# Two layers of a hybrid trunk: the step-size chain's products issued with the z products

## The chip, the cores and the metric

The kernel runs on one core of a Trainium2 chip. The metric is the device time of one execution in microseconds, over several runs. Four compute engines matter here: TensorE (PE) multiplies matrices, VectorE (DVE) and ScalarE (ACT) do the elementwise work, and SyncE (SP) starts the DMAs that bring the weights from HBM. GpSimd (POOL) has almost nothing to do.

## The reference

Each of two layers is a half-step SwiGLU feed-forward block, a mixer and a second feed-forward block, on 256 tokens of width 1024 in float32. The mixer has one input projection, whose columns are z, xBC, dt, q, k and v. Of its two halves the first is a Mamba-2 scan in chunks of 128 tokens, and the step sizes, with which this change deals, belong to it (cut to what matters):

```python
xbc = jax.nn.silu(causal_depthwise_conv(xbc, conv_w[i], conv_b[i]))
dt = jax.nn.softplus(dt_raw + dt_bias)            # 16 heads, 256 tokens
a = -jnp.exp(a_log)
adt = dt * a
a_cum = jnp.cumsum(adt, axis=-1)                  # within a chunk
lmat = jnp.exp(segment differences of a_cum, causal)
y_diag = cb * lmat * X                            # X = x * dt
decay_states = jnp.exp(a_cum[..., -1:] - a_cum)   # the kernel's dec, first chunk
states = Bc, decay_states, X
y_off = Cc, previous state, exp(a_cum)            # the kernel's dec, second chunk
```

The other half is attention: q and k are normalised per head with an RMS norm, scores are masked in three dilated windows, and their softmax weighs v. Both halves side by side go through the output projection.

## The kernel before, in words

Every big product is made three times, from a high and a low part of the weights and of the activations (L250 to L252, or the same sum in another order). The weights come in halves of 128x1024. For each half ScalarE casts the high part (L166, `wh`) and VectorE subtracts it from the weights to get the low part (L168, `wl`). The mixer's halves go through a ring of five slots, r0 to r4. In the stage of q, k and v a half serves 12 products of 512 columns, four halves serve a block of 512 output columns, and a slot is written again five halves later, so the cast of a half waits for the last product that reads the slot's old content.

The order of the mixer's products is: z with dt (the z stage), xBC with the convolutions, then first halves of q, k and v, second halves of q, k and v, and the output projection. Each block of q, k or v goes into a pair of PSUM tiles (`mm_pair`), one tile for each half of the tokens. Work that depends on finished blocks runs in generators ("threads"): `spawn` puts one on a list, `tick` (once for a step of the products) lets each go on to its next `yield`, and `after(events)` yields until the named events have been added. The SSD work (`group_in`, `decay_mask`, `group_out`), the normalising of q and k (`qk_norm_T`) and the attention (`head_pair`) are such threads. The order of the source is a priority only: a scheduler then places each instruction in its engine's queue by its own estimate of when its operands are there, so that an instruction can stand ahead of one that the source gives earlier.

The step-size chain (`step_sizes`, L521) computes dt as a softplus by an exponential and a series on VectorE (L525 to L541), adt and its high and low parts (L543 to L546), two small products that sum adt along the tokens (`pd`, L550 and L551), the exponential of the sums (`dec`, L552), and the first chunk's product of dec and dt (`dtd`, L553). The event "dt" lets `group_in` go on to `xe` (L619), and `decay_mask` begin. In `qk_norm_T`, L736 and L737 make the sums of squares, `rsqrt` (L223 to L236) their reciprocal roots, L742 the normalised q or k, and L749 transposes these on TensorE.

```python
def after(*evs):
    while not all(e in events for e in evs):
        yield 1
```

Of the kernel before, what the change touches and what calls it, by code (L numbers as in the profile page):

```python
# [18 lines left out]
AF = mybir.ActivationFunctionType  # L19
# [33 lines left out]
def tile_hybrid_trunk(ctx: ExitStack, tc: tile.TileContext, x, w_ffn_in, w_ffn_down, w_z, w_dtz,  # L53
                      w_xbc, w_qkv, w_out, norms, conv_wb, head_par, qk_norm, consts, out):
    nc = tc.nc
    vec, act, pool, pe = nc.vector, nc.scalar, nc.gpsimd, nc.tensor
# [151 lines left out]
# [3 lines that stand above are left out]
# [290 lines left out]
    def mixer(layer, xT, xn, norm, tail):  # L501
# [15 lines left out]
        dec = sm.tile(sh, F32, tag="dec", name="dec")  # L517
# [2 lines left out]

        def step_sizes():  # L521

            yield from after(*[f"xbc{j}" for j in range(8)])
            e = sm.tile(sh, F32, tag="sp_e", name="sp_e")
            vec.scalar_tensor_tensor(e, u, -1.0, u, op0=OP.mult, op1=OP.min)  # L525
            first = act.activation(e, e, AF.Exp)
            with tc.issue_after(first.ins):
                act.activation(ea, hpar[:, layer, 1, :], AF.Exp)
            yield 1
            s = sm.tile(sh, F32, tag="sp_s", name="sp_s")  # L530
            vec.tensor_scalar(s, e, 2.0, None, op0=OP.add)
            vec.reciprocal(s, s)
            vec.tensor_tensor(s, s, e, op=OP.mult)
            s2 = sm.tile(sh, F32, tag="sp_s2", name="sp_s2")
            vec.tensor_tensor(s2, s, s, op=OP.mult)
            a = sm.tile(sh, F32, tag="sp_a", name="sp_a")
            vec.tensor_scalar(a, s2, 1.0 / 15, None, op0=OP.mult)
            for n in (13, 11, 9, 7, 5, 3):
                vec.scalar_tensor_tensor(a, a, 1.0 / n, s2, op0=OP.add, op1=OP.mult)
            vec.scalar_tensor_tensor(a, a, 1.0, s, op0=OP.add, op1=OP.mult)  # L540
            vec.tensor_scalar(dt, u, 0.0, None, op0=OP.max)  # L541
            vec.scalar_tensor_tensor(dt, a, 2.0, dt, op0=OP.mult, op1=OP.add)
            vec.scalar_tensor_tensor(adt, dt, -1.0, ea[:, None, :].to_broadcast(sh),  # L543
                                     op0=OP.mult, op1=OP.mult)
            vec.tensor_copy(adh, adt)
            vec.tensor_tensor(adl, adt, adh.bitcast(F32), op=OP.subtract)  # L546
            yield 1

            pd = pt.tile(sh, F32, tag="s", name="pd")
            pe.matmul(pd[:, 0, :], low, adt[:, 0, :], start=True, stop=True)  # L550
            pe.matmul(pd[:, 1, :], tri, adt[:, 1, :], start=True, stop=True)  # L551
            act.activation(dec, pd, AF.Exp)  # L552
            vec.tensor_tensor(dtd, dec[:, 0, :], dt[:, 0, :], op=OP.mult)  # L553
            events.add("dt")

        a2, z1 = [st.take(), st.take()], [st.take(), st.take()]
        for t in range(2):
# [6 lines left out]
            unit_first(256, xT, t, z1, p1[:, :256])  # L564
            act.activation(zs[t][:, 512:768], p1[:, :256], AF.Silu)
        spawn(step_sizes())
        pz = mm_pair("pz", 512)
        unit_tok(512, 2, xT, pz)
# [385 lines left out]
```

## Time and profile before

| | |
|---|---|
| median of 3 runs | 1228.69 us (1228.65 to 1229.54) |
| profiled execution | 1229.02 us |
| its span on the core | 1227.2 us |
| TensorE busy | 1219.2 us |
| VectorE busy | 780.7 us |
| ScalarE busy | 686.2 us |
| mean granted clock of TensorE | 0.999 |

The profiled execution is one run; its span is the time between the first and the last instruction in the trace. A busy share is a mean over stages. Layer 1's z stage lies from about 197 to 221.5 us of the span, its convolutions to 269, its stage of q, k and v to 376.5, and the output projection to 428; layer 2's stage of q, k and v lies from 876 to 983. Times below are us from the span's start.

### The profile page before, as it was taken

The numbers are of one execution on the slowest core, as the hardware profiler recorded it, in microseconds if no ns is written. First come the engines' busy times: TensorE is split into PE (matmuls) and PEld (weight loads), VectorE is DVE, ScalarE is ACT, GpSimd is POOL, SyncE is SP. The second block draws the span as 40 slices with busy tenths as digits, with TensorE's granted clock in tenths as the row PEclk, the third lists the DMA queues.
The fourth block names the chain that finished last, engine by engine and source line by source line (L and its number), as shares of the span: only waits on it lengthen the run. The fifth ranks groups of instructions, "written<-read, shape, count | busy, mean of one in ns | idle before, by whom it ended". The sixth has DMA issues, their size and how long they took to land.

```text
span 1227.2 us, 16729 instructions
## 1 busy us (share of the span) xinstructions
PE 1219.2 (99%) x6191; PEld 1018.2 (83%) x6191; DVE 780.7 (64%) x1389; ACT 686.2 (56%) x1118; POOL 7.3 (1%) x14
## 2 busy tenths in 40 slices
PE   9999999999999999999999999999999999999998
PEld 6888888998877888888888888889988778888887
DVE  6755546788796586554385554478887875755541
ACT  6654435677866465544364543366769674644440
POOL 0000000000000000000000000000000000000000
PEclk9999999999999999999999999999999999999999
DMA  8855553654334466555456554645533344755550
GB/s 297 265 181 187 185 192 105 205 178 136 111 126 135 156 222 206 188 185 181 150 202 211 189 184 142 208 143 190 183 120 104 120 130 144 268 185 184 188 171 35
DMA packets 58833, 211.48 MB, mean 172 GB/s; under 512 B 6784, under 2 KB 7040, under 8 KB 58752
## 3 DMA queue, kind: packets, MB, share of 16 engines
q1 hardware_dynamic: 58032, 208.24, 50.2%
q0 software_dynamic: 576, 2.10, 0.5%
q8 instruction: 49, 0.80, 0.3%
q14 instruction: 32, 0.26, 0.1%
q10 hardware_dynamic: 144, 0.08, 0.0%
HBM read 209.34 MB, written 1.05 MB: 171 GB/s over the span
## 4 chain that ended last, share of the span: by engine, by line
PE 97%; DVE 1%; ACT 1%; DMA 1%; issue 0%; SPq 0%
PE pgu L250 13%; PE pgu L252 13%; PE pgu L251 13%; PE acc L250 9%; PE acc L251 9%; PE acc L252 9%; PE pq L252 3%; PE pq L250 3%; PE pq L251 3%; PE pc L252 3%; PE pc L250 3%; PE pc L251 3%; PE tr L467 2%; PE pz L250 1%; PE pz L251 1%; PE psc L783 1%
## 5 line engine op out<-in xcount | busy, mean ns | idle before, releaser
L168 DVE TENSOR_TENSOR wl<-w,wh 128x1024 fp32r<-128x1024 f32 x268 | 327.4, 1224 | 190.7 <-ACT wh L166 188.1
L166 ACT CAST wh<-w 128x1024 fp32r<-128x1024 f32 x268 | 280.6, 1052 | 225.1 <-PE pgu L252 71.8
L168 DVE TENSOR_TENSOR we<-w,we 128x1024 fp32r<-128x1024 f32 x124 | 151.2, 1225 | 126.1 <-ACT we L166 124.7
L166 ACT CAST we<-w 128x1024 fp32r<-128x1024 f32 x124 | 130.1, 1054 | 131.5 <-PE pgu L252 62.6
L250 PE MATMUL pgu<-wh,xTh 128*128 128x512 f32 x384 | 151.9, 396 | 0.1
L251 PE MATMUL pgu<-wl,xTh 128*128 128x512 f32 x384 | 149.6, 390 | 0.0
L252 PE MATMUL pgu<-wh,xTl 128*128 128x512 f32 x384 | 149.3, 390 | 0.0
L250 PE MATMUL pgu<-we,xTh 128*128 128x512 f32 x312 | 123.3, 395 | 0.0
L251 PE MATMUL pgu<-we,xTh 128*128 128x512 f32 x312 | 121.5, 390 | 0.0
L252 PE MATMUL pgu<-we,xTl 128*128 128x512 f32 x312 | 121.4, 390 | 0.0
L252 PEld LDWEIGHTS pgu<-wh,xTl 128*128 128x128 f32 x384 | 72.1, 188 | 15.3
L250 PEld LDWEIGHTS pgu<-wh,xTh 128*128 128x128 f32 x384 | 72.1, 188 | 15.0 <-ACT xTh L286 0.8
L251 PEld LDWEIGHTS pgu<-wl,xTh 128*128 128x128 f32 x384 | 72.2, 188 | 14.3
L250 PE MATMUL pq<-wh,xTh 128*128 128x512 f32 x192 | 78.8, 410 | 0.0
L252 PE MATMUL pq<-wh,xTl 128*128 128x512 f32 x192 | 78.2, 407 | 0.0
L251 PE MATMUL pq<-wl,xTh 128*128 128x512 f32 x192 | 78.2, 407 | 0.0
L250 PE MATMUL pc<-xTh,wh 128*128 128x256 f32 x256 | 72.9, 285 | 0.0
L252 PE MATMUL pc<-xTh,wl 128*128 128x256 f32 x256 | 72.4, 283 | 0.0
L251 PE MATMUL pc<-xTl,wh 128*128 128x256 f32 x256 | 72.4, 283 | 0.0
L252 PEld LDWEIGHTS pgu<-we,xTl 128*128 128x128 f32 x312 | 58.6, 188 | 12.5
L250 PEld LDWEIGHTS pgu<-we,xTh 128*128 128x128 f32 x312 | 58.6, 188 | 11.9 <-ACT xTh L286 0.3
L251 PEld LDWEIGHTS pgu<-we,xTh 128*128 128x128 f32 x312 | 58.6, 188 | 11.7
(209 smaller groups left out, 2259.7 us busy)
## 6 DMA issues: line engine op xcount, KB each, us to landing
w<-in_w_ffn_in_dram SPq DMA_DIRECT2D x176, 512.0 KB, 4.6
w<-in_w_ffn_down_dram SPq DMA_DIRECT2D x88, 512.0 KB, 3.7
w<-in_w_qkv_dram SPq DMA_DIRECT2D x48, 512.0 KB, 3.6
w<-in_w_xbc_dram SPq DMA_DIRECT2D x32, 512.0 KB, 4.3
w<-in_w_out_dram SPq DMA_DIRECT2D x32, 512.0 KB, 3.7
w<-in_w_z_dram SPq DMA_DIRECT2D x12, 512.0 KB, 4.9
w<-in_w_dtz_dram SPq DMA_DIRECT2D x4, 544.0 KB, 5.1
nw<-in_norms_dram POOLq DMA_DIRECT2D x4, 512.0 KB, 4.6
```

What stands on the lines that cost most here:

```text
L166: self.high = act.copy(h, src)
L168: self.low = vec.tensor_tensor(l, src, h.bitcast(F32), op=OP.subtract)
L250: pe.matmul(o, ah, bh, start=first, stop=False)
L251: pe.matmul(o, ah, bl, start=False, stop=False)
L252: guard["pe"] = pe.matmul(o, al, bh, start=False, stop=last)
L467: pe.transpose(p[:, i, tok(t)], h[:, t, i * 128:(i + 1) * 128], ident)
L783: pe.matmul(p[:, 0:256], qT[:, pr, 128:256], kz[:, pr % 4, i, :], start=True, stop=True)
```

## The change

The wait for the convolutions' events no longer stands at the head of the chain but between the pd products and the exponential of dec. The sums are copied out of PSUM by VectorE, and the exponential works in place on the copy.

```diff
@@ -520,7 +520,6 @@
 
         def step_sizes():
 
-            yield from after(*[f"xbc{j}" for j in range(8)])
             e = sm.tile(sh, F32, tag="sp_e", name="sp_e")
             vec.scalar_tensor_tensor(e, u, -1.0, u, op0=OP.mult, op1=OP.min)
             first = act.activation(e, e, AF.Exp)
@@ -549,7 +548,9 @@
             pd = pt.tile(sh, F32, tag="s", name="pd")
             pe.matmul(pd[:, 0, :], low, adt[:, 0, :], start=True, stop=True)
             pe.matmul(pd[:, 1, :], tri, adt[:, 1, :], start=True, stop=True)
-            act.activation(dec, pd, AF.Exp)
+            vec.tensor_copy(dec, pd)
+            yield from after(*[f"xbc{j}" for j in range(8)])
+            act.activation(dec, dec, AF.Exp)
             vec.tensor_tensor(dtd, dec[:, 0, :], dt[:, 0, :], op=OP.mult)
             events.add("dt")
 
```

Lines from L524 to L550 of the new file are the old L525 to L551; the copy is L551, the exponential L553, dtd L554, and later lines are the old number plus 1.

What this makes of the queues differs in three places. ScalarE's queue in the z stage of layer 1, before the change (`ea` is the exponential of a_log, `zv` the activation of z, ACT_TABLE_LOAD the loading of a function's table):

```order
L565 ACT_TABLE_LOAD
L565 ACTIVATE zv<-pz_1705 128x256
L166 CAST wh<-w 128x1024
L528 ACT_TABLE_LOAD
L528 ACTIVATE ea<-hpar 128x16
L166 CAST wh<-w 128x1024 x2
L570 ACT_TABLE_LOAD
L570 ACTIVATE zv<-pz_1781 128x512
L166 CAST wh<-w 128x1024
```

And after it:

```order
L566 ACT_TABLE_LOAD
L566 ACTIVATE zv<-pz_1705 128x256
L527 ACT_TABLE_LOAD
L527 ACTIVATE ea<-hpar 128x16
L166 CAST wh<-w 128x1024 x2
L553 ACTIVATE dec<-dec 128x32
L166 CAST wh<-w 128x1024
L571 ACT_TABLE_LOAD
L571 ACTIVATE zv<-pz_1781 128x512
```

The exponential of dec now stands in the z stage, behind that of ea and with no load of its own, and ea with its load stands one cast earlier.

The pd products move on TensorE from the first block of q to the place behind the 25th of the 48 z products of 512 columns (counted without dt's).

VectorE's queue in the stage of q, k and v, at the normalising of the second half of q (`qn`), before the change:

```order
L236 SCALAR_TENSOR_TENSOR rs_y<-rs_a,rs_y 128x16
L768 TENSOR_SCALAR sc<-sc,den 128x256
L742 TENSOR_TENSOR qn<-pq_3033,rs_y 128x512
L742 TENSOR_TENSOR qn<-pq_3034,rs_y 128x512
L768 TENSOR_SCALAR sc<-sc,den 128x128
L768 ISA sc,nm<-psc,cc 128x128
L768 ISA nm 128x1
L226 TENSOR_SCALAR rs_a<-rs_m 128x8
L168 TENSOR_TENSOR wl<-w,wh 128x1024
```

And after it, where L743 is the old L742:

```order
L235 SCALAR_TENSOR_TENSOR rs_a<-rs_a,rs_m 128x16
L229 TENSOR_TENSOR rs_a<-rs_a,rs_m 128x8
L769 ISA sc,nm<-psc,cc 128x128
L769 ISA nm 128x1
L236 SCALAR_TENSOR_TENSOR rs_y<-rs_a,rs_y 128x16
L231 TENSOR_SCALAR rs_b<-rs_a 128x8
L168 TENSOR_TENSOR wl<-w,wh 128x1024
L743 TENSOR_TENSOR qn<-pq_3049,rs_y 128x512
L743 TENSOR_TENSOR qn<-pq_3050,rs_y 128x512
L769 RECIPROCAL den<-den 128x2
```

The two products that make qn stood ahead of a half of weights (L168) with other work between; now the L168 stands directly ahead of them.

TensorE's queue where the second half of v begins, before the change:

```order
L250 MATMUL pq_3221<-wh,xTh 128x512
L251 MATMUL pq_3221<-wl,xTh 128x512
L252 MATMUL pq_3221<-wh,xTl 128x512
L749 MATMUL tr<-first_c,qn 128x128 x4
L250 MATMUL pq_3500<-wh,xTh 128x512
L749 MATMUL tr<-first_c,qn 128x128 x4
L251 MATMUL pq_3500<-wl,xTh 128x512
```

And after it:

```order
L250 MATMUL pq_3247<-wh,xTh 128x512
L251 MATMUL pq_3247<-wl,xTh 128x512
L252 MATMUL pq_3247<-wh,xTl 128x512
L250 MATMUL pq_3501<-wh,xTh 128x512
L251 MATMUL pq_3501<-wl,xTh 128x512
L252 MATMUL pq_3501<-wh,xTl 128x512
```

The transposes of qn (L749), between which the first product of v stood, are no longer there; they come later.

## Rows read from the trace of the kernel before

**Rows 1.** The page: busy time of each engine; the chain that ended last.
```profile
PE 1219.2 (99%) x6191; PEld 1018.2 (83%) x6191; DVE 780.7 (64%) x1389; ACT 686.2 (56%) x1118; POOL 7.3 (1%) x14
...
PE 97%; DVE 1%; ACT 1%; DMA 1%; issue 0%; SPq 0%
```

**Rows 2.** Busy time by stretch (columns in the first line): both q/k/v stages.
```profile
core 0: us, PE busy (x) PEld busy (x) DVE busy (x) ACT busy (x) POOL busy (x), PEclk, DMA share, GB/s
269.00:376.50 107.50, 106.75 (x567) 86.50 (x565) 85.48 (x231) 83.93 (x193) 0.53 (x1) 1.00 0.38 128
876.00:983.00 107.00, 106.23 (x563) 86.07 (x562) 84.96 (x228) 83.55 (x193) 0.00 (x0) 1.00 0.38 124
```

**Rows 3.** Timeline (start us, us, engine, line, operation), layer 1, q/k/v stage, ACT and DVE.
```profile
278.37 1.28 ACT L552 ACT_TABLE_LOAD   x1
278.38 1.23 DVE L168 TENSOR_TENSOR wl<-w,wh 128x1024 fp32r<-128x1024 f32 x1 [1.49 <-ACT wh L166]
...
279.66 0.20 ACT L552 ACTIVATE dec<-pd 128x32 f32<-128x32 f32 x1
...
279.89 0.18 DVE L553 TENSOR_TENSOR dtd<-dec,dt 128x16 f32<-128x16 f32 x1 [0.28 <-ACT dec L552]
```

**Rows 4.** Timeline of the z stage, layer 1: ACT, DVE and PE.
```profile
214.20 0.39 ACT L565 ACTIVATE zv<-pz 128x256 f32<-128x256 f32 x1
...
215.54 1.28 ACT L528 ACT_TABLE_LOAD   x1
...
215.80 0.19 DVE L540 SCALAR_TENSOR_TENSOR sp_a<-sp_a,sp_s 128x32 f32<-128x32 f32 x1
...
216.10 0.39 PE L250 MATMUL pz<-wh,xTh 128*128 128x512 f32 x1
...
216.83 0.22 ACT L528 ACTIVATE ea<-hpar 128x16 f32<-128x16 f32 x1
...
217.33 0.19 DVE L543 SCALAR_TENSOR_TENSOR adt<-dt,ea 128x32 f32<-128x32 f32 x1
```

**Rows 5.** Timeline of PE where the second value half begins, layer 1.
```profile
352.35 0.40 PE L251 MATMUL pq<-wl,xTh 128*128 128x512 f32 x1
...
352.58 0.40 PE L252 MATMUL pq<-wh,xTl 128*128 128x512 f32 x1
...
353.25 0.66 PE L749 MATMUL tr<-first_c,qn 128*128 128x128 f32 x4 [0.27 <-DVE qn L742]
```

**Rows 6.** Timeline of DVE and ACT at the same place.
```profile
350.53 1.22 DVE L168 TENSOR_TENSOR wl<-w,wh 128x1024 fp32r<-128x1024 f32 x1
...
351.67 0.17 DVE L235 SCALAR_TENSOR_TENSOR rs_a<-rs_a,rs_m 128x16 f32<-128x16 f32 x1
...
352.51 1.28 DVE L742 TENSOR_TENSOR qn<-pq,rs_y 128x512 f32<-128x512 f32 x2
...
353.01 1.05 ACT L166 CAST wh<-w 128x1024 fp32r<-128x1024 f32 x1
...
354.18 1.22 DVE L168 TENSOR_TENSOR wl<-w,wh 128x1024 fp32r<-128x1024 f32 x1
```

**Rows 7.** Timeline of PE and ACT, two halves of weights earlier.
```profile
344.04 0.39 PE L252 MATMUL pq<-wh,xTl 128*128 128x512 f32 x1
...
344.47 1.05 ACT L166 CAST wh<-w 128x1024 fp32r<-128x1024 f32 x1 [1.74 <-PE pq L252]
```

**Rows 8.** Timeline of PE at two later places of layer 1.
```profile
359.90 0.39 PE L251 MATMUL pq<-wl,xTh 128*128 128x512 f32 x1
360.49 0.41 PE L695 MATMUL tr<-first_c,zv 128*128 128x128 f32 x2 [0.20 <-DVE zv L689]
...
374.43 0.39 PE L252 MATMUL acc<-wh,yT 128*128 128x512 f32 x1
375.09 0.70 PE L783 MATMUL psc<-kz,qT 128*128 128x256 f32 x2 [0.27 <-ACT kz L754]
```

**Rows 9.** Timeline of PE in layer 2, where the second value half begins.
```profile
959.55 0.40 PE L252 MATMUL pq<-wh,xTl 128*128 128x512 f32 x1
960.22 0.66 PE L749 MATMUL tr<-first_c,qn 128*128 128x128 f32 x4 [0.27 <-DVE qn L742]
```

## The prediction

> **What bounds the kernel now.** I read the summary of the engines first. TensorE is busy for 99% of the span, and the chain that ended last is 97% TensorE [rows 1]. So a change saves time only where it takes away a wait of TensorE or a TensorE instruction, and costs time wherever it adds one, since no other engine has slack to give back. Next I read busy time by stage: in the stage of the query, key and value products (the q/k/v stage) TensorE is idle by the records for about 0.75 us in either layer, out of 107 us, while ScalarE and VectorE are busy for some four fifths of it [rows 2]. In that stage VectorE and ScalarE serve everything at once (halves of weights, the SSD work, attention), each strictly in the order of its queue, so the order within a queue can matter more than the amount of work. Last I read the timeline where the changed instructions stand, and then each pause of TensorE in the q/k/v stage: from start to start two 512-column products stand 0.23 us apart (352.35 and 352.58, [rows 5]), and whatever is longer is a pause.
>
> **What the change moves.** The diff reads as if the chain's products moved into the z stage and the exponential stayed. The order of the instructions says more. The vector part of the chain and both of its first exponentials already run in the z stage before the change (from 214 us on, [rows 4]), although the source asks for the convolutions first; only the pd products, the exponential of dec with its table load, and the dtd product run in the q/k/v stage [rows 3]. After the change all of these are in the z stage, the exponential and dtd too: the wait for the convolutions sets a place in the source and not in the queue.
>
> **Removed from the q/k/v stage, per layer.** (1) Two small pd products of TensorE. They stand between two big products before and after, so what they take is only paid elsewhere: 0. (2) On ScalarE one table load of 1.28 us and an exponential of 0.20; on VectorE waits of 1.49 and 0.28 us and 0.18 us of dtd [rows 3]. Neither engine is what TensorE waits for at that point, so by itself this is 0 too. The load is not saved either: the order shows six loads per layer before and after, as the Exp of the decay masks now needs its own.
>
> **Added in the z stage, per layer.** One VectorE copy of 128x32 (0.19 us, as its neighbours of that shape, L540 and L543) and the exponential, now with no load of its own since it stands behind that of ea. The pd products read adt and wait for it. In the order ea stands one cast earlier: its load can start when the zv activation ends, 214.20 + 0.39 = 214.59; it takes 1.28, and ea (0.22) is there at about 216.1. VectorE's L540 starts at 215.80 and L542, L543 follow at about 0.23 us each, now with no half of weights between, so adt is there at about 216.45. TensorE comes to the pd products one product after 216.10, at about 216.32 [rows 4]. A pause of 0.2 us, with bounds of 0 (if TensorE is a little later) and 1.5 (if the ea load stays where it was, behind a cast: adt then comes at 217.33 + 0.19, and 1.2 us of pause results). I take 0.2, because the new order has the load ahead of that cast. The halves of weights that stand behind the pd copy on VectorE are late by about 0.5 us; the first is wanted by TensorE only in the next stage, some 4 us later: 0.
>
> **Moved in the q/k/v stage, per layer.** This is the term that decides. With dtd ready early, the SSD work begins about 14 products (3 us) sooner, and all that follows stands otherwise on VectorE and TensorE until the end of the stage. I compared the new order with the old one place by place for a wait of TensorE on something that stands late in a queue. One stands out: the first product of the second value half, which I call V1. Its PSUM tiles are those of the second query half, so it needs the two L742 products (the query's normalising, L743 in the new file) to have read them. Before, the two stand ahead of the next half of weights on VectorE: L742 starts at 352.51 and L168 at 354.18 [rows 6]. After, that L168 stands directly ahead of them. This L168 subtracts what the cast L166 made; the cast writes the slot that the last product ahead of V1 reads, and it starts when that product is done (353.01, the product having started at 352.58 for 0.40). So TensorE's last product, the cast, L168, L742 and V1 become one chain with nothing beside it:
> - last product's start to the cast's start: 344.04 to 344.47, 0.43 [rows 7]
> - the cast's start to L168's start: 353.01 to 354.18, 1.17 [rows 6]
> - L168's start to the next on VectorE: 350.53 to 351.67, 1.14 [rows 6]
> - L742's start to what TensorE was waiting for: 352.51 to 353.25, 0.74 [rows 5, 6]
>
> Sum 3.48 us from start to start, where 0.23 is normal: a pause of 3.25. Before there was a pause at this place too: 352.58 to 353.25 is 0.67, so 0.44 [rows 5]. The step costs 3.25 - 0.44 = 2.81 us. Its bounds: the full 3.25 if the old 0.44 shows up elsewhere, and 2.4 if the 0.43 ahead of the cast falls away (the ends of products are modelled).
>
> Given back in that stage: two other pauses of TensorE, 359.90 to 360.49 (waits for zv, 0.36) and 374.43 to 375.09 (waits for kz, 0.43) [rows 8]. During a pause of 3 us at V1 ScalarE and VectorE can catch up, and both waits can go: at most 0.79. But the key transposes and zv are queued otherwise as well, with margins of 0.3 to 0.9 us by my working, so some of it can come back as other pauses. I take 0.5.
>
> Per layer: 0.2 + 2.81 - 0.5 = 2.5. Layer 2 has the same order at the same place and the same pause, 959.55 to 960.22, so 0.67 [rows 9]. Two layers: 5.0. The profiled execution took 1229.02 (span 1227.2 and 1.8 around it), which gives 1234.0; the median of the runs is 0.33 lower, so the forecast is 1233.7.
>
> **Rivals.**
> - No change (1227.5 to 1231): the cast of that L168 is released by an earlier product, so that L168 has long been done when TensorE comes to V1. Then the pause at V1 is the old one or none, and the sum is 0.2 - 0.5 per layer and up to +1. For it: in [rows 6] the cast has no recorded wait. Against: the same cast two halves before has one, of 1.74 us, released by the last product of a half [rows 7], and slots repeat with the halves.
> - Faster: all three pauses of the stage go, because the SSD work is out of the way 3 us sooner and L742 is ready before the half that now stands ahead of it. The place is again V1; the price is 0.44 + 0.36 + 0.43 = 1.23 per layer, 2.46 for both, which with 0.4 lost at pd gives 1226.6. It decides if the cast can run one half (12 products, 2.8 us) earlier. For it: VectorE waits for 1.49 us and 0.28 us just where the load went [rows 3]. Against: that idle time lies 70 us before V1, and by the order the gain of 14 products has shrunk to 2 by the eighth output product of the SSD work.
> - A larger loss: TensorE's clock falls in the pause. In every row of stages here the granted clock is 1.00, its level of 2.4 GHz, but no pause of that length stands in these stages [rows 2]. If products ran at 1.2 GHz for as long as the pause lasted, 3.25 us, half of that time is lost, 1.6 per layer, and the time is 1233.7 + 3.2 = 1236.9. The Trainium skill (TensorE: Matmul & The Clock Gate, Part 1) says that the array's clock is throttled unless recent activity releases it; no row of this case shows a fall.
> - The change does what it says, and the exponential stays behind the convolutions: then the SSD work begins as before, and only the pd pause of 0.2 per layer is added: 1229.1. The order speaks against it.
>
> **Chances.** The forecast (pause at V1 as worked out, 1231.9 to 1235.6: per layer 2.4 - 0.79, and 3.25 + 0.2 with nothing given back) 0.73; the larger loss 0.11; no change 0.09 and the change as described 0.02; faster 0.05. About 0.2%, 2.5 us, is what a measurement of this kernel can tell from no change, so slower by more than that holds 0.84, within it 0.11, faster 0.05. The range reaches below the forecast's own to 1230.4, for the upper part of the no-change case, and above it to 1237.0, which takes in the larger loss, and 1.2 us at pd in both layers beside the forecast (1233.7 + 2.0 = 1235.7).
>
> **What would show it.** In the profile after, a pause of TensorE of 3.0 to 3.5 us ahead of the first product of the second value half in both layers, with the L742 line as its releaser and L168 directly ahead on VectorE, whose own wait is for the cast and the cast's for TensorE; the exponential of dec in the z stage with no load; a pause ahead of pd of 0 to 0.5; the pauses at zv and kz shorter. The prediction is wrong if V1 starts within 1 us of the product ahead of it, if the pause is there and an equal time is missing elsewhere in the stage, or if the granted clock of the stage is under 0.98.

## The result, and the profile after

The changed kernel takes 1240.88 us (median of 5 runs, 1238.85 to 1242.36) against 1228.69 us before: slower by 12.2 us, ratio 1.0097 (95% interval 1.0085 to 1.0108). That lies above the range of 1230.4 to 1237.0. In a later comparison the same kernel took 1239.66 against 1228.59 us, ratio 1.0088 (1.0075 to 1.0102). The direction was forecast, and the size was not: 5 us were forecast, 11 to 12 were lost.

The profiled execution took 1241.09 us. Its page (the span; the busy times; TensorE's granted clock in 40 slices, in tenths) answers to [rows 1]:

```profile
span 1239.2 us, 16732 instructions
...
PE 1224.5 (99%) x6191; PEld 1021.0 (82%) x6191; DVE 779.3 (63%) x1391; ACT 686.0 (55%) x1118; POOL 9.8 (1%) x14
...
PEclk9999999999989999999999999999999999999999
```

TensorE's busy time has risen by 5.3 us although it has the same number of instructions, and one slice of the clock is below 9. So some products ran slower than before. Busy time by stretch, both q/k/v stages (the columns are those of [rows 2]):

```profile
270.50:378.00 107.50, 104.25 (x536) 83.60 (x536) 82.58 (x224) 80.80 (x188) 0.53 (x1) 0.97 0.38 127
883.50:990.00 106.50, 103.22 (x537) 82.85 (x536) 82.55 (x224) 80.94 (x188) 0.00 (x0) 0.98 0.38 123
```

In either layer TensorE now is idle for 3.3 us in place of 0.75, and the granted clock is 0.97 and 0.98 where it was 1.00. The place is the one that the prediction named. Timeline of TensorE, ScalarE and VectorE of layer 1 where the second value half begins, as in [rows 5, 6]:

```profile
354.43 0.40 PE L252 MATMUL pq<-wh,xTl 128*128 128x512 f32 x1
...
354.86 1.04 ACT L166 CAST wh<-w 128x1024 fp32r<-128x1024 f32 x1 [1.63 <-PE pq L252]
...
355.44 0.17 DVE L236 SCALAR_TENSOR_TENSOR rs_y<-rs_a,rs_y 128x16 f32<-128x16 f32 x1
...
355.94 1.23 DVE L168 TENSOR_TENSOR wl<-w,wh 128x1024 fp32r<-128x1024 f32 x1 [0.25 <-ACT wh L166]
...
357.08 1.28 DVE L743 TENSOR_TENSOR qn<-pq,rs_y 128x512 f32<-128x512 f32 x2
...
357.91 0.77 PE L250 MATMUL pq<-wh,xTh 128*128 128x512 f32 x1 [3.09 <-DVE qn L743]
...
358.48 0.63 PE L251 MATMUL pq<-wl,xTh 128*128 128x512 f32 x1
...
358.90 0.63 PE L252 MATMUL pq<-wh,xTl 128*128 128x512 f32 x1
```

The last key product starts at 354.43, its cast at 354.86 (0.43 later), L168 at 355.94 (1.08), L743 at 357.08 (1.14), the first value product at 357.91 (0.83): 3.48 from start to start, a pause of 3.25 us. The prediction had the same sum, by two differences that cancel: it put 1.17 where 1.08 was measured and 0.74 where it was 0.83. The rows behind it show what it had left to a rival: the next products start 0.42 us apart and not 0.23, and last 0.63. Granted clock in stretches of 2 us around the place (columns: length, TensorE's busy time and instructions, granted clock, DMA share, GB/s):

```profile
core 0: us, PE busy (x), PEclk, DMA share, GB/s
354.00:356.00 2.00, 0.83 (x4) 1.00 0.82 260
356.00:358.00 2.00, 0.09 (x1) 0.70 0.52 201
358.00:360.00 2.00, 2.00 (x5) 0.50 0.73 240
360.00:362.00 2.00, 2.00 (x6) 0.50 0.09 31
362.00:364.00 2.00, 2.00 (x7) 0.59 0.00 0
364.00:366.00 2.00, 2.00 (x15) 1.00 0.00 0
```

The clock falls to 0.50, which is 1.2 GHz, inside the pause (between 356 and 358 us), and is back at 1.00 some 6 us after the first value product. Layer 2 has the same pause, 967.36 to 970.85, and there too the products slow down:

```profile
967.36 0.40 PE L252 MATMUL pq<-wh,xTl 128*128 128x512 f32 x1
...
970.85 0.47 PE L250 MATMUL pq<-wh,xTh 128*128 128x512 f32 x1 [3.09 <-DVE qn L743]
...
971.15 0.57 PE L251 MATMUL pq<-wl,xTh 128*128 128x512 f32 x1
...
971.52 0.63 PE L252 MATMUL pq<-wh,xTl 128*128 128x512 f32 x1
```

In the z stage (layer 1, as [rows 4]):

```profile
216.76 0.22 ACT L527 ACTIVATE ea<-hpar 128x16 f32<-128x16 f32 x1
...
216.96 0.39 PE L250 MATMUL pz<-wh,xTh 128*128 128x512 f32 x1
217.18 0.19 DVE L542 SCALAR_TENSOR_TENSOR adt<-dt,ea 128x32 f32<-128x32 f32 x1
...
217.42 0.40 PE L549 MATMUL pd<-adt,cc 128*128 128x16 f32 x2
...
217.89 0.48 PE L251 MATMUL pz<-wl,xTh 128*128 128x512 f32 x1
...
218.21 0.39 PE L252 MATMUL pz<-wh,xTl 128*128 128x512 f32 x1
...
218.77 0.22 ACT L553 ACTIVATE dec<-dec 128x32 f32<-128x32 f32 x1
```

TensorE could have started the pd products at 217.19 and starts them at 217.42, when adt is there: a pause of 0.23. The exponential of dec follows at 218.77 with no table load. From 216.96 to 218.21 pass 1.25 us in which two z products start; that is 0.79 more than their 0.46.

Where the 12.0 us between the two spans lie, from the starts of the stages in the two timelines (for the q/k/v stage with the output projection, the share of the clock is the difference to the same stage of the kernel with the pause partly filled, below):

| | layer 1 | layer 2 |
|---|---|---|
| ahead of the first big product | +0.89 | |
| z stage | +0.79 | +0.81 |
| q/k/v stage and output projection, at full clock | +2.83 | +2.82 |
| the same, products at 1.2 GHz | +2.65 | +1.55 |
| feed-forward blocks | -0.30 | 0 |

The 0.89 is not put down to the change: the first big product waits for a cast of weights that waits for a first transfer, and in the other profiles of the changed order it started at 8.9 to 9.2 us, as before (9.06).

### The profile page after: what moved, and what is told of

Same layout as the page of the kernel before. It is cut to its first block, busy times and chain, and to the rows that moved or that the text cites. A ratio compares the mean times of both kernels' runs of the same rounds, so it can differ in the third digit from the quotient of the medians.

```text
span 1239.2 us, 16732 instructions
## 1 busy us (share of the span) xinstructions
PE 1224.5 (99%) x6191; PEld 1021.0 (82%) x6191; DVE 779.3 (63%) x1391; ACT 686.0 (55%) x1118; POOL 9.8 (1%) x14
## 4 chain that ended last, share of the span: by engine, by line
PE 95%; ACT 2%; DVE 1%; DMA 1%; issue 0%; SPq 0%; ACTq 0%; DVEq 0%
PE pgu L250 13%; PE pgu L252 13%; PE pgu L251 13%; PE acc L250 9%; PE acc L251 9%; PE acc L252 9%; PE pq L252 3%; PE pq L250 3%; PE pq L251 3%; PE pc L252 2%; PE pc L250 2%; PE pc L251 2%; PE tr L467 2%; PE py L669 1%; PE psc L784 1%; DMA w<-in_w_ffn_in_dram 1%
## 5 line engine op out<-in xcount | busy, mean ns | idle before, releaser
L168 DVE TENSOR_TENSOR wl<-w,wh 128x1024 fp32r<-128x1024 f32 x268 | 327.4, 1224 | 183.6 <-ACT wh L166 181.1
L168 DVE TENSOR_TENSOR we<-w,we 128x1024 fp32r<-128x1024 f32 x124 | 151.0, 1224 | 125.3 <-ACT we L166 123.9
L250 PE MATMUL pq<-wh,xTh 128*128 128x512 f32 x192 | 81.6, 425 | 6.2 <-DVE qn L743 6.2
```

Source lines behind the costliest of these rows:

```text
L168: self.low = vec.tensor_tensor(l, src, h.bitcast(F32), op=OP.subtract)
L250: pe.matmul(o, ah, bh, start=first, stop=False)
```

## Experiments

All times are medians; the kernel before ran beside each group, at 1228.59 to 1228.71 us.

**Filling the pause.** Is the low clock a cost of its own, or does it fill time in which TensorE would have waited anyway? Products of zeros, added to the last key sums, stand between the last key product and the first value product; all other queues keep the changed kernel's order. The edit, shortened:

```diff
+                    if a == KT // kper - 1:
+                        for i in range(extra):
+                            pe.matmul(o[1], zero_r, zeros of 512 columns, start=False, stop=i == extra - 1)
                     st.done(hf)
...
-            unit_tok(512, 2, xT, pp)
+            unit_tok(512, 2, xT, pp, 13 if b and which == 1 else 0)
```

13 products. Expected:

> The changed kernel with 13 more products of 512 columns of zeros on TensorE, in each layer, between the last product of the second key half and the first of the second value half (they add zero to the key's sums). All queues are otherwise in the changed kernel's order. Theory A (the lost time is the pause of 3.25 us and, behind it, products at 1.2 GHz): the products fill the pause, the first value product starts when it did, 3.5 us behind the last key product, and the granted clock stays 1.00; the time falls by the 4.3 us that the low clock cost in the profile (2.64 and 1.60), from 1240.9 to about 1236.6. Theory B (the clock is beside the point, since the products at 1.2 GHz only use up time in which TensorE would have waited for weights or PSUM anyway): the time stays within 1 us of 1240.9 whatever the clock does.

Measured: 1236.13 us (1235.88 to 1238.08), clock 1.00 throughout, ratio 1.0063 (1.0050 to 1.0075). Theory A had 1236.6. The added products cost nothing, and the time falls.

6 products. Expected:

> The same with 6 products of zeros in place of 13, so that TensorE works for the first 1.4 us of the pause and stands still for the last 1.9. Theory A: the first value product starts as late as before; if 1.9 us of standing still is not enough for the clock to fall, 1236.6 as with 13; if it falls all the same, between 1238 and 1241. Theory B: within 1 us of 1240.9.

Measured: 1236.09 us (1235.82 to 1236.75), ratio 1.0060 (1.0047 to 1.0073). TensorE's timeline and clock:

```profile
353.50 0.40 PE L254 MATMUL pq<-wh,xTl 128*128 128x512 f32 x1
...
353.74 1.47 PE L376 MATMUL pq<-zero_r 128*128 128x512 bf16 x6
...
356.99 0.47 PE L252 MATMUL pq<-wh,xTh 128*128 128x512 f32 x1 [1.78 <-DVE qn L748]
```

```profile
354.00:356.00 2.00, 1.21 (x6) 1.00 0.88 260
356.00:358.00 2.00, 1.01 (x5) 1.00 0.54 203
358.00:360.00 2.00, 2.00 (x10) 1.00 0.44 166
```

The first value product starts 3.49 us behind the last key product as before; of this TensorE stands still for about 1.9 us, and the clock stays at 1.00.

3 products. Expected:

> The changed kernel with 3 products of zeros in the pause, in place of 6 or 13: TensorE works for 0.7 us of it and stands still for some 2.6. Theory A: the first value product starts 3.5 us behind the last key product as before. With 1.9 us of standing still the clock stayed at 1.00; if it stays here too, 1236.1; if it falls as with 3.25 us, 1238 to 1241; if in some executions only, a wider spread between these.

Measured: 1239.74 us (1239.22 to 1240.44), beside 1239.66 for the changed kernel itself on the same chip: nothing gained.

```profile
354.39 0.40 PE L254 MATMUL pq<-wh,xTl 128*128 128x512 f32 x1
...
354.63 0.82 PE L376 MATMUL pq<-zero_r 128*128 128x512 bf16 x3
...
357.87 0.47 PE L252 MATMUL pq<-wh,xTh 128*128 128x512 f32 x1 [2.42 <-DVE qn L748]
...
359.18 0.63 PE L254 MATMUL pq<-wh,xTl 128*128 128x512 f32 x1
...
359.61 0.63 PE L252 MATMUL pq<-wh,xTh 128*128 128x512 f32 x1
```

```profile
356.00:358.00 2.00, 0.13 (x1) 1.00 0.60 234
358.00:360.00 2.00, 2.00 (x7) 0.74 0.73 250
360.00:362.00 2.00, 2.00 (x6) 0.50 0.06 20
```

Here TensorE stands still for some 2.6 us. The clock is still 1.00 while it does, and in this layer falls about a microsecond after the products begin. Theory B falls: with the pause in place and the clock at 1.00 the kernel is 4.8 us faster than the changed kernel's first median and 3.6 us faster than its later one (1239.66 - 1236.1). That later median was taken on another chip than these fillings; the kernel before took 1228.59 us beside the one and 1228.62 beside the other. On the fillings' own chip the moved wait without the copy, below, is 2.9 us slower than they are (1238.97).

**Which edit.** The moved wait without the copy:

```diff
-            vec.tensor_copy(dec, pd)
             yield from after(*[f"xbc{j}" for j in range(8)])
-            act.activation(dec, dec, AF.Exp)
+            act.activation(dec, pd, AF.Exp)
```

> The wait for the convolutions moved as in the change, but without the copy: the exponential reads the sums in PSUM, as before the change. Apart from the copy all queues stand as in the changed kernel. Theory A: the same pause and the same low clock, so 1240.9 within 1 us. Theory C (the copy and the in-place exponential cost time of their own, through VectorE in the z stage): 1238 or less.

Measured: 1238.97 us (1238.59 to 1240.36), 1.9 less than the changed kernel's first median: between the two theories. Repeated beside the changed kernel on one chip:

> The changed kernel itself once more, beside the gate alone and the short filling on one chip. Theory A: between 1238.5 and 1241, and the profile starts its first big product at about 9.0 us of the span, as all others did, and not at 9.95: the 0.9 us there came from one execution's first transfers and not from the change.

> The moved wait without the copy once more, beside the changed kernel on the same chip. Theory A: both differ by less than 1 us, since the 1.9 us between their first medians came from how long the clock stayed low after the pause (14 and 11 products at half speed in the one, 2 and 11 in the other). Theory C (the copy costs time): again 1.5 to 2 us less than the changed kernel.

Measured: 1239.66 us (1238.82 to 1240.43) for the changed kernel, 1239.72 (1238.81 to 1240.51) without the copy. The copy costs nothing; the place of the wait alone makes the loss. The count of 2 slow products in the expectation was wrong: in the profile without the copy they cost 1.56 and 1.44 us (stages of 109.93 and 109.82 against 108.37 and 108.38 with the clock at 1.00), against 2.65 and 1.55 in the changed kernel's. How long the clock stays low differs from one execution to the next. The first product of the changed kernel's new profile starts at 9.16 us, not 9.95, but that execution loses 0.8 us later in the first feed-forward block, where its granted clock is 0.68 from 10 to 12 us and 0.50 from 12 to 14. The profile with 3 products has the same fall there; the kernel before and the kernels with 6 and 13 products have none.

The copy alone, with the wait at the head:

```diff
-            act.activation(dec, pd, AF.Exp)
+            vec.tensor_copy(dec, pd)
+            act.activation(dec, dec, AF.Exp)
```

> The kernel before with the copy and the exponential in place alone; the wait for the convolutions stays at the head of the chain. The pd products, the copy, the exponential with its table load and dtd stay in the q/k/v stage, and the normalising products of the second query half stay ahead of the half of weights. Theory A: within 0.7 us of 1228.6. Theory C (the copy costs time of its own): 1230 or more.

Measured: 1229.05 us (1228.88 to 1229.20), ratio 1.0002 (0.9993 to 1.0011): no difference.

**The suspected order alone, in the kernel before.** The chain stays; L742 of the second query half is put behind the half of weights (shortened):

```diff
             rr = rsqrt(ss, [128, 2, 8])
+            if b and not which:
+                yield 7
...
+                with tc.issue_after(st.low.ins) if b and not which else nullcontext():
                     vec.tensor_tensor(q, pp[t]..., rr[:, t, :, None]...)
```

> The kernel before, its step-size chain as it was, with one thing added: the two normalising products of the second query half (L742) are put behind the half of weights whose cast waits for the last key product, as in the changed kernel. Theory A: the same pause and the same fall of the clock without the chain's move: ahead of the second value half TensorE stands still for about 3.5 us (3.7 less what lies beside it) instead of 0.44, and runs at 1.2 GHz for some 4 to 7 us behind it; per layer 3.1 for the pause, 1.6 to 2.6 for the clock, up to 0.8 given back by the waits at zv and kz: 1228.6 + 2 x 4.5 = 1237.6, between 1235.5 and 1239.5. Theory D (the pause alone is harmless, and the loss needs the earlier SSD work of the changed kernel around it): 1231 or less.

Measured: 1237.78 us (1236.94 to 1239.05), ratio 1.0071 (1.0058 to 1.0085), where 1237.6 was expected. Timeline of its layer 1:

```profile
352.60 0.40 PE L252 MATMUL pq<-wh,xTl 128*128 128x512 f32 x1
...
353.04 1.04 ACT L166 CAST wh<-w 128x1024 fp32r<-128x1024 f32 x1
...
354.11 1.23 DVE L168 TENSOR_TENSOR wl<-w,wh 128x1024 fp32r<-128x1024 f32 x1
...
355.39 0.68 DVE L745 TENSOR_TENSOR qn<-pq,rs_y 128x512 f32<-128x512 f32 x1
...
356.22 0.47 PE L250 MATMUL pq<-wh,xTh 128*128 128x512 f32 x1 [3.23 <-DVE qn L745]
...
357.69 0.63 PE L250 MATMUL pq<-wh,xTh 128*128 128x512 f32 x1
...
358.11 0.63 PE L251 MATMUL pq<-wl,xTh 128*128 128x512 f32 x1
```

A pause of 3.39 us, and 1.5 us behind it products 0.42 us apart. The order at this one place makes 9.1 us (1237.78 - 1228.71) without any move of the step-size chain. V1 starts ahead of the second of the two normalising products, so it waits for the first alone. Theory D falls.

**The order set right in the changed kernel.** First, that half of weights goes behind L743 (one edge, from the second query half's last normalising product to the L168 of the output projection's first half; the line that sets it):

```diff
-                with behind("vec"):
+                with tc.issue_after(self.q1.ins) if self.piece in OUT0 and not self.sub else behind("vec"):
                     self.low = vec.tensor_tensor(l, src, h.bitcast(F32), op=OP.subtract)
```

> The changed kernel with one thing in the order set by hand: the half of weights that stood ahead of the two normalising products of the second query half (L743 in the changed kernel) now stands behind them. Theory A: the pause ahead of the second value half shrinks, but not to the 0.44 us of before, since the reciprocal root that L743 reads is itself ready only about 1.0 us after the last key product (355.44 against 354.43 in the changed kernel's trace): about 1.7 us remain, too short for the clock to fall; 1240.9 - 2 x 1.55 - 4.3 = 1233.5. Theory B: 1240.9 - 3.1 = 1237.8. If the place of that half of weights has nothing to do with the loss: 1240.9.

Measured: 1233.12 us (1232.99 to 1234.53), ratio 1.0039 (1.0027 to 1.0052), where 1233.5 was expected. The pause is now this:

```profile
353.54 0.40 PE L253 MATMUL pq<-wh,xTl 128*128 128x512 f32 x1
...
354.70 1.29 DVE L744 TENSOR_TENSOR qn<-pq,rs_y 128x512 f32<-128x512 f32 x2
...
355.54 0.48 PE L251 MATMUL pq<-wh,xTh 128*128 128x512 f32 x1 [1.60 <-ACT sc L772]
```

It is 1.77 us (1.82 in layer 2), and the clock stays at 1.00. The profile puts the wait down to ScalarE's work on the scores, which the value product does not read. Its start lies 0.84 us behind that of the normalising products (here L744), where the changed kernel has 0.83, so these are taken as what it waits for. So the half of weights was 1.5 us of the pause; the rest is the late reciprocal root (its last step starts at 354.50, 0.96 behind the last key product), whose steps share VectorE with the scores and with another root.

Then the whole chain of the second query half (L736 to L743) gets a higher priority, in the changed kernel and in the one before:

```diff
+            with tc.high_priority(offset=URGENT) if b and not which else nullcontext():
                 (sums of squares, rsqrt, the two products)
```

> The changed kernel with the same priority. Theory A: no pause at the second value half, so no fall of the clock: the time with the pause filled, 1236.1, less 2 x 3.25, so 1229.6. What is then left against the kernel before, about 1 us, is the z stage (0.8 per layer more than before) less the pd products that the later stage no longer has. Theory E (the new order loses time in many small waits as well): 1231 to 1233.

> The kernel before, with the second query half's sums of squares, reciprocal root and normalising products given a higher priority, so that its L742 stands some 30 instructions earlier on VectorE. Theory A: the old pause of 0.44 us at the second value half goes, in both layers, and nothing else of size changes: 1228.6 - 0.9 = 1227.7. If the work that is pushed back makes waits of its own: 1228.6 to 1231.

Measured: 1230.15 us in the changed kernel (ratio 1.0012, 1.0003 to 1.0021), 1228.85 in the one before (ratio 1.0000, 0.9991 to 1.0009). In the changed kernel 9.5 to 10.7 us come back with one priority, and the time lies between theory A's 1229.6 and theory E's 1231, nearer to A. Some 1.4 us are left against the kernel before: its z stage is 0.79 and 0.79 us longer in the two layers, its q/k/v stage with the output projection 0.1 and 0.2 shorter. In the kernel before nothing is gained, and theory A's 1227.7 is not reached, though the three waits of TensorE that [rows 5, 8] show are gone; its waits by line that are left are these (waited for: us in total, times, longest us):

```profile
PE idle_out L849 <- DVE idle L844: 1.2, 1, 1.2
PE pgu L348 <- ACT wh L166: 1.1, 1, 1.1
PE tr L276 <- DMA first_c<-in_consts_dram: 0.3, 1, 0.3
```

The q/k/v stage with the output projection takes 161.18 us against 161.11 before (layer 1): about 0.3 less between neighbouring big products, about 0.3 more in the stretches that hold small ones. Why those stretches grew by as much as the waits had taken stays open. No version here beats the kernel before.

## Why the prediction was wrong, step by step

- **The place and the mechanism** were right: V1 waits for L743, L743 stands behind L168, L168 waits for a cast, the cast for the last key product. Step 3.48, pause 3.25, and net 2.81 per layer, as measured in both layers, though two of its four parts were off by 0.09 each and cancelled by luck.
- **The exponential is not held back**, ea is one cast earlier, and the pd products wait 0.23 us: as forecast (0.2).
- **The step that failed: "a pause of 3.25 us" was priced as 3.25 us.** The sum held only rows at full clock, and the fall of the clock stood as a rival of chance 0.11 because no row before showed one. But no pause before in these stages was longer than 0.44 us, so the rows were silent on 3.25 and no evidence against a fall. And the trace of the kernel before does hold a fall, at its very end, where TensorE's last product ends at 1223.2 us (columns as in the table of the clock above):

```profile
1223.30:1225.60 2.30, 0.00 (x0) 1.00 0.30 114
1225.70:1227.20 1.50, 0.00 (x0) 0.50 0.00 0
```

TensorE stood still for some 2.4 us there, less than the 3.25 that were forecast, and the clock went to 0.50. "No row of this case shows a fall" held for the rows that were read and not for the trace. In the stage the clock costs 4.2 us in the changed kernel's first profile and 3.2 in its second, and 2.9 to 4.8 by the medians with the pause filled. The rival had the right mechanism and 3.2 us; its time at 1.2 GHz, as long as the pause, was a guess that came near. The prediction's own sign of being wrong, a granted clock of the stage under 0.98, came true in layer 1 (0.97).

- **"Given back 0.5"** failed as well. The waits at zv and kz did go, as forecast (from 270 to 437 us the only wait of TensorE that the changed kernel's profile lists is the one for L743), and the stage is none the shorter: at full clock it is 2.83 longer, the V1 step alone. The urgent chain in the kernel before shows the same: waits of 0.4 us go and the time stays. That is 2 x 0.5 of the error; what took up the time of these waits stays open, as above.
- **The pd products "only paid elsewhere"**: the z stage grew by 0.80 us per layer and not by 0.2, since the two products cost 0.57 where they are now (0.80 less the wait of 0.23), and the stage that lost them is hardly shorter for it: in the kernel before they took about 0.4 there (the big products around them start at 276.87 and 277.46), but with the urgent chain and no pause it takes 161.03 us against 161.18 with the urgent chain in the kernel before. That is 2 x 0.6 of the error.

At full clock the forecast of 5.0 becomes 5.0 + 1.0 + 1.2 = 7.2, and the kernel with 6 products in the pause is 1236.09 - 1228.62 = 7.5 above the one before. The first measurement missed the forecast by 7.2 us (1240.88 - 1233.7): 4.2 for the clock, 1.0 and 1.2 for these two terms, and 0.9 of a late start in that profile, 7.3 together. In the later comparison the kernel lost 11.1 us (1239.66 - 1228.59); the clock's 3.2 in its profile and the 7.5 make 10.7, and 11.5 with the 0.8 that this profile lost at the start.

## What to carry to other kernels

When a change reorders queues, look for the instruction that frees a buffer and what now stands ahead of it in its queue; a half of weights that waits for the last product makes a serial chain through three engines. Price a pause of TensorE of some microseconds with the slow products behind it, as long as no row shows a pause of that length at full clock, and look for such a row in the whole trace, its two ends included. A cheap test tells the two apart: fill the pause with products of zeros.

## What the runs showed of the hardware that was not expected

- In the stage of q, k and v, standing still for 1.8 to 1.9 us left the granted clock at 1.00; 2.6, 3.25 and 3.39 us took it to 0.50 in both layers of every profile. The fall comes inside the pause in one place (layer 1 of the changed kernel, between 356 and 358 us) and up to 1.5 us after the products have begun again in others, and costs 1.4 to 2.7 us each time. The Trainium skill (TensorE: Matmul & The Clock Gate, Part 1) says that the array runs at the lower clock unless recent activity releases it; these runs agree, with 0.50 for 1.2 GHz.
- The length of standing still does not settle it alone. At the kernel's start TensorE waits for the first weights: 1.9 us in the changed kernel's second profile and 1.8 us with 3 products, and there the clock falls to 0.50 some 1.6 to 1.8 us after the products have begun; in the changed kernel's first profile it waits 2.2 us and the clock stays at 1.00. What makes the difference stays open.
- Products of zeros in a pause kept the clock at 1.00 where enough of them were there, and cost no time: 13 and 6 of them give 1236.13 and 1236.09 us. With 3 it fell (1239.74).
